# Half-contraction feed-forward chunks, two chunks per PSUM bank, and norm1 modulation on TensorE in one layer of a hybrid attention/S5 decoder

## The chip, the cores and the metric

The kernel runs on one core of a Trainium2 chip. The metric is the device time in microseconds (us) of one execution, as the median of several runs. Engines are named as in the profile: PE is TensorE (PEld its weight loads), DVE is VectorE, ACT is ScalarE, POOL is GpSimd, SP issues the transfers.

## The reference, cut to what matters

One layer, 256 tokens, width 2048, float32:

```
mod = silu(c) @ w_ada + b_ada                  # w_ada: 2048 x 12288, 100 MB
sh1, sc1, g1, sh2, sc2, g2 = split(mod, 6)
h = rms_norm(x, norm1_g) * (1 + sc1) + sh1
q, k, v, u = split(h @ w_in)                   # 2048 x 4096
attn = dilated_attention(qk_norm(q), qk_norm(k), v)
y = gelu(s5_mixer(u, ...)); ssm = y * sigmoid(y @ w_glu + b_glu)
x = x + g1 * (concat(rms_norm(attn), rms_norm(ssm)) @ w_out)     # 2048 x 2048
h2 = rms_norm(x, norm2_g) * (1 + sc2) + sh2
out = x + g2 * (square(relu(h2 @ w_ff1)) @ w_ff2)                # 2048 x 8192 x 2048
```

## The kernel before, in words

Activations lie transposed: channels on the 128 partitions, 256 tokens along the free dimension. Every product is made of float32 values split into a high and a low part of type fp32r: high x high, high x low and low x high. Weights come in tiles of 512 KB (128 partitions x 2 x 512). `raw` (L176) issues each transfer on SP's queue into one of five `raw` buffers; `split` (L172) makes the high part `wh` on ScalarE and the low part `wl` on VectorE, three buffers of each.

**The modulation.** w_ada has 24 blocks of 512 columns. Blocks 0 to 3 are sh1, 4 to 7 sc1, 8 to 11 g1, 12 to 15 sh2, 16 to 19 sc2, 20 to 23 g2. `ada_pieces` (L241) does a block in four pieces of 1 MB, which are two `raw` tiles each, or one larger tile where a ring of other buffers is set. A block in `PE_BLOCKS` (L42) goes to TensorE: per piece four matmuls against `cpad` at 32 columns each (L249, eight records per piece), and at the end a copy of the rows on ScalarE and column sums (L260). Any other block goes to VectorE: per raw tile one product with `cbc` whose sum is read out (L158). `ADA_ORDER` (L43) is the order of the blocks. Pieces are put between other work by `pump(n)` and `pump_at(i)` (L280, L581): `pump_at(i)` adds PUMPS[i] to a running sum and issues as many whole pieces; `until` stops it at that many pieces of the 96.

**The order of the work.** Norm 1; 8 pieces; `make_h(0)`; then the 32 blocks of w_in with S5 preparation, `make_h(1)` to `make_h(3)` and the scan between them (L607 to L650); attention and w_glu; `branch_scale`. w_out follows in two passes (L865 and L878) of eight `w_out_pair`, over the S5 half and the attention half of the contraction. A pair takes two weight tiles and two PSUM banks: each chunk of 128 output channels has a bank, whose columns 0 to 255 hold high times high plus low times high, and columns 256 to 511 high times low. Two additions per chunk on VectorE (L156, out XT, which is `z`) then bring both into z. The second pass also squares z on ScalarE (L883) and sums the squares with a matmul against ones (L886).

Then norm 2: the inverse root on VectorE (n2), its broadcast by matmul (L817), and `make_h2(kg)` (L899) for four chunks of channels each: on VectorE v = z * g2c * r2 (L905), on ScalarE the high part (L907), on VectorE the low part (L908). `make_h2(kg)` first pumps until 56 + 8 kg pieces, as it needs the blocks 12 + kg and 16 + kg.

The feed-forward part has 32 pairs of w_ff1 (64 chunks) with four weight tiles each, and w_ff2 in four groups G of eight pairs. `ff1_first` runs the first four pairs together in all eight banks (four `tr`, four `acc`), so that each quarter of h2 is used as soon as it is made. A pair's result is taken out in `ff1_out`: a copy on ScalarE and an addition on VectorE for each chunk, then the squared relu, the high part and the low part.

Tile places the instructions: it follows the program's order as priority but lets an instruction run ahead where its engine would be idle in its own simulated timeline. Each engine then takes its instructions strictly in the order so fixed.

Of the kernel before, what the change touches and what calls it, by code (L numbers as in the profile page):

```python
# [9 lines left out]
F32 = mybir.dt.float32  # L10
# [3 lines left out]
ALU = mybir.AluOpType  # L14
PSUM = bass.MemoryType.PSUM

P = 128
SEQ = 256
# [7 lines left out]
NB = 512  # L26
RAW = 5
RINGS = (('raw',), ('raw',), ('T0', 'PD', 'raw', 'raw'), ('T0', 'raw', 'raw'), ('U', 'raw'), ('WB0', 'U', 'raw', 'raw'))
PUMPS = (2.5, 2.75, 1.0, 1.5, 0.75, 0.75, 1.5, 1.25, 1.0, 2.0, 0.25, 2.75, 1, 0.75)

COLS = {}
_o = 0
# [6 lines left out]
NCOLS = _o  # L39

SUB = [0, 2, 1, 3]
PE_BLOCKS = (0, 4, 5, 7, 10, 11, 12, 16)  # L42
ADA_ORDER = (4, 0, 5, 1, 6, 2, 7, 3, 8, 9, 10, 11, 12, 16, 13, 17, 14, 18, 15, 19, 20, 21, 22, 23)  # L43


# [71 lines left out]
class _K:  # L117
# [5 lines left out]
    def t(self, tag, shape, dt=F32, bufs=1):  # L123
        self.n += 1
        return self.sb.tile(list(shape), dt, name=f"{tag}_{self.n}", tag=tag, bufs=bufs)
# [5 lines left out]
    def tr(self):  # L131
        self.n += 1
        return self.ps.tile([P, NB], F32, name=f"tr_{self.n}", tag="tr", bufs=4)
# [7 lines left out]
    def add(self, out, a, b, eng=None):  # L141
        return self.tt(out, a, b, ALU.add, eng)

    def sub(self, out, a, b, eng=None):
        return self.tt(out, a, b, ALU.subtract, eng)
# [8 lines left out]
    def stt(self, out, a, s, b, op0, op1, accum=None):  # L154
        if accum is None:
            self.nc.vector.scalar_tensor_tensor(out, a, s, b, op0=op0, op1=op1)  # L156
        else:
            self.nc.vector.scalar_tensor_tensor(out, a, s, b, op0=op0, op1=op1, accum_out=accum)  # L158

    def copy(self, out, a, scale=1.0):  # L160
        self.nc.scalar.activation(out, a, AF.Copy, scale=scale)  # L161
# [36 lines left out]
def _body(nc, tc, I, out, sb, ps):  # L198
    k = _K(nc, tc, I, out, (sb, ps))
    t, tr = k.t, k.tr  # L200
    mul, add, sub, ts, stt, copy = k.mul, k.add, k.sub, k.ts, k.stt, k.copy
    mm = nc.tensor.matmul
# [21 lines left out]
    cpad = t("cpad", [P, 16, 32])  # L224
# [356 lines left out]
    def pump_at(i, until=96):  # L581
        state["due"] += PUMPS[i]
        n = int(state["due"] + 1e-6)
        state["due"] -= n
        pump(n, until)
# [250 lines left out]
    def load_p(src):  # L836
        w = k.raw(src)
        hi = t("wh", [P, 2, 4, P], F32R, bufs=3)
        lo = t("wl", [P, 2, 4, P], F32R, bufs=3)
        flat = lambda v: v.rearrange("p e k n -> p e (k n)")  # L840
        k.split(flat(hi), flat(lo), w)
        return hi, lo

    def pair_part(pp, src, xs, first, last):
        hi, lo = load_p(src)
        for e in range(2):
            for kk in range(4):
                mm(pp[e], hi[:, e, kk], xs[kk].rearrange("p s n -> p (s n)"), start=first and kk == 0, stop=False)  # L848
            for kk in range(4):
                mm(pp[e][:, 0:SEQ], lo[:, e, kk], xs[kk][:, 0], start=False, stop=last and kk == 3)  # L850


    def w_out_pair(half, x8, np_):
        pp = [k.acc(), k.acc()]
        for kg in range(2):
            xs = [x8[:, 4 * kg + kk] for kk in range(4)]
            pair_part(pp, I["w_out"][np_, 2 * half + kg], xs, kg == 0, kg == 1)
        for e in range(2):
            c = 2 * np_ + e
            for s in (1, 0):  # L860
                stt(
                    z[:, c], pp[e][:, SEQ * s : SEQ * s + SEQ], mod[:, 32 + c : 33 + c], z[:, c], ALU.mult, ALU.add
                )

    for np_ in range(8):  # L865
        w_out_pair(1, xss, np_)
# [11 lines left out]
    for np_ in range(8):  # L878
        w_out_pair(0, xat, np_)
        if np_ % 2:  # L880
            pump_at(12, 80)
        sq = nsq[np_ // 4][:, 2 * (np_ % 4) : 2 * (np_ % 4) + 2]
        nc.scalar.activation(sq, z[:, 2 * np_ : 2 * np_ + 2], AF.Square)  # L883
        for e in range(2):
            for m in range(2):
                mm(  # L886
                    pn2[:, m : m + 1], sq[:, e, P * m : P * m + P], ones,
                    start=np_ + e + m == 0, stop=np_ + e + m == 9,
                )
# [9 lines left out]
    def make_h2(kg):  # L899
        pump(99, until=56 + 8 * kg)  # L900
        c4 = slice(4 * kg, 4 * kg + 4)
        stt(g2c[:, c4], mod[:, 64 + 4 * kg : 68 + 4 * kg], 1.0, col["n2g"][:, c4], ALU.add, ALU.mult)
        for c in range(4 * kg, 4 * kg + 4):
            v = nsq[c // 8][:, c % 8]
            stt(v, z[:, c], g2c[:, c : c + 1], r2, ALU.mult, ALU.mult)  # L905
            sh = mod[:, 48 + c : 49 + c]
            nc.scalar.activation(h2[c][:, 0], v, AF.Identity, bias=sh)  # L907
            stt(h2[c][:, 1], v, sh, h2[c][:, 0].bitcast(F32), ALU.add, ALU.subtract)  # L908


    y2 = [t("WB2", [P, 8, SEQ]), t("WB3", [P, 8, SEQ])]
    y2 = [y2[c // 8][:, c % 8] for c in range(16)]
    slots = [t(s, [P, 4, 2, SEQ], F32R) for s in ("HA", "U", "WB1", "HB", "V", "WB0")]
    xq = t("QK", [P, 2, 4, 2, SEQ], F32R)
    slots += [xq[:, 0], xq[:, 1]]

    def ff1_part(pp, np_, kg):
        pair_part(pp, I["w_ff1"][np_, kg], h2[4 * kg : 4 * kg + 4], kg == 0, kg == 3)

    def ff1_out(pp, np_):  # L920
        aa = slots[np_ // 2 % 8][:, 2 * (np_ % 2) : 2 * (np_ % 2) + 2]
        v = t("rows", [P, 2, SEQ], bufs=2)
        for e in range(2):
            copy(v[:, e], pp[e][:, SEQ : 2 * SEQ])
            add(v[:, e], pp[e][:, 0:SEQ], v[:, e])
        stt(v, v, 0.0, v, ALU.max, ALU.mult)
        copy(aa[:, :, 0], v)
        sub(aa[:, :, 1], v, aa[:, :, 0].bitcast(F32))

    def ff1(np_):  # L930
        pp = [k.acc(), k.acc()]
        if np_ % 2 == 0:
            pump(1)
        for kg in range(4):
            ff1_part(pp, np_, kg)
        ff1_out(pp, np_)

    def ff1_first():
        pps = [[tr(), tr()], [tr(), tr()], [k.acc(), k.acc()], [k.acc(), k.acc()]]
        for kg in range(4):  # L940
            make_h2(kg)
            for np_ in range(4):
                ff1_part(pps[np_], np_, kg)
                if kg < 3:
                    pump_at(13, 80)
        for np_ in range(4):
            ff1_out(pps[np_], np_)

    def ff2(G, np_):
        pp = [k.acc(), k.acc()]  # L950
# [14 lines left out]
            if G == 3:  # L965
                nc.sync.dma_start(out[c], y)

    ff1_first()
    for np_ in range(4, 8):
        ff1(np_)  # L970
    for G in range(4):
        if G < 3:
            for np_ in range(2):
                ff1(8 * G + 8 + np_)
        if G == 3:
            pump(99)
            for c in range(16):
                stt(y2[c], y2[c], mod[:, 80 + c : 81 + c], z[:, c], ALU.mult, ALU.add)
        for np_ in range(8):
            ff2(G, np_)  # L980
        if G < 3:
            for np_ in range(2, 8):
                ff1(8 * G + 8 + np_)
# [21 lines left out]
```

## Time and profile before

| | us |
|---|---|
| median of 3 runs | 1285.88 |
| lowest, highest | 1280.72, 1296.6 |
| profiled execution | 1299.06 |
| its span | 1297.3 |
| PE busy | 1198.6 (92%) |
| PEld busy | 993.7 (77%) |
| DVE busy | 921.8 (71%) |
| ACT busy | 582.0 (45%) |
| moved by DMA | 299.59 MB, mean 231 GB/s |

The profiled execution is one execution, and 1% above the median of the runs shown. Shares over the whole span say little here, as the stretches differ; the rows below are by stretch. A busy TensorE isn't TensorE at its peak: matmuls overlap, so their cost is read from start to start.

### The profile page before, as it was taken

What the parts mean: (1) busy time and instruction counts of PE and PEld (TensorE: products, weight loads), DVE (VectorE), ACT (ScalarE), POOL (GpSimd) and SP (SyncE); (2) the same over time, 40 slices, a digit from 0 to 9 for tenths busy, and PEclk for the clock granted to TensorE, in tenths of its full rate; (3) what the DMA queues carried; (4) which work ended last, traced back from release to release, by engine and by line L of the source; (5) the groups of instructions that cost most, each with busy time, mean ns of one, the idle gap of its engine ahead of it and who ended that gap; (6) DMA issues with size and microseconds to landing.
All of it is one profiled execution on the core that took longest, in us unless ns stands there. A gap on an engine that the chain in (4) does not pass through costs nothing.

```text
span 1297.3 us, 17972 instructions
## 1 busy us (share of the span) xinstructions
PE 1198.6 (92%) x6818; PEld 993.7 (77%) x6818; DVE 921.8 (71%) x1520; ACT 582.0 (45%) x807; POOL 13.0 (1%) x12
## 2 busy tenths in 40 slices
PE   5777999998987977949999999999999999999998
PEld 1355778865677866838888888888888888888887
DVE  9687678899555898877865556765566666667764
ACT  3579544322275533324544444443344443344432
POOL 3000000000000000000000000000000000000000
PEclk9788999999688897969999999999999999999999
DMA  9687898888544486748766666765677666667763
GB/s 345 228 271 259 337 341 314 286 313 289 196 149 162 149 302 213 255 154 275 242 220 188 189 217 224 248 192 184 190 233 239 224 183 191 205 235 248 241 211 96
DMA packets 82166, 299.59 MB, mean 231 GB/s; under 512 B 9120, under 2 KB 11424, under 8 KB 80288
## 3 DMA queue, kind: packets, MB, share of 16 engines
q1 hardware_dynamic: 82080, 298.45, 69.2%
q8 instruction: 53, 0.87, 0.3%
q14 instruction: 33, 0.27, 0.1%
HBM read 296.31 MB, written 2.10 MB: 230 GB/s over the span
## 4 chain that ended last, share of the span: by engine, by line
PE 76%; DVE 8%; DMA 7%; ACT 6%; issue 2%; SPq 0%; DVEq 0%; ACTq 0%
PE acc L848 37%; PE acc L850 18%; DMA raw<-w_ada 6%; PE acc L194 4%; PE acc L195 4%; PE acc L193 4%; DVE wl L136 2%; PE tr L249 2%; DVE raw L158 2%; PE acc L690 1%; ACT wh L161 1%; PE tr L553 1%; PE acc L686 1%; ACT TO L161 1%; PE tr L848 1%
## 5 line engine op out<-in xcount | busy, mean ns | idle before, releaser
L136 DVE TENSOR_TENSOR wl<-raw,wh 128x1024 fp32r<-128x1024 f32 x360 | 439.8, 1223 | 260.6 <-ACT wh L161 259.6
L161 ACT ACTIVATE wh<-raw 128x1024 fp32r<-128x1024 f32 x360 | 381.3, 1060 | 505.5 <-PE acc L848 347.2
L158 DVE SCALAR_TENSOR_TENSOR raw<-raw,cbc 128x1024 f32<-128x1024 f32 x112 | 136.6, 1222 | 53.7 <-DMA raw<-w_ada 53.1
L848 PE MATMUL acc<-CA,wh 128*128 128x512 f32 x608 | 167.0, 397 | 2.5 <-DVE XT L156 2.0
L848 PE MATMUL acc<-TO,wh 128*128 128x512 f32 x480 | 132.0, 396 | 0.6 <-DVE rows L136 0.6
L848 PE MATMUL acc<-QK,wh 128*128 128x512 f32 x384 | 107.4, 402 | 13.1 <-DVE QK L136 13.1
L848 PEld LDWEIGHTS acc<-CA,wh 128*128 128x128 f32 x608 | 104.7, 189 | 16.7 <-issue 2.2
L850 PEld LDWEIGHTS acc<-CA,wl 128*128 128x128 f32 x608 | 92.4, 188 | 13.1
L850 PE MATMUL acc<-CA,wl 128*128 128x256 f32 x608 | 96.1, 281 | 0.0
L848 PEld LDWEIGHTS acc<-TO,wh 128*128 128x128 f32 x480 | 82.5, 189 | 11.7 <-PE acc L850 0.8
L848 PEld LDWEIGHTS acc<-QK,wh 128*128 128x128 f32 x384 | 67.4, 193 | 22.4 <-issue 13.3
L850 PEld LDWEIGHTS acc<-TO,wl 128*128 128x128 f32 x480 | 73.3, 188 | 10.6
L850 PE MATMUL acc<-TO,wl 128*128 128x256 f32 x480 | 76.1, 281 | 0.0
L848 PE MATMUL acc<-WB,wh 128*128 128x512 f32 x256 | 69.8, 394 | 0.0
L850 PEld LDWEIGHTS acc<-QK,wl 128*128 128x128 f32 x384 | 58.3, 189 | 7.7
L850 PE MATMUL acc<-QK,wl 128*128 128x256 f32 x384 | 60.3, 279 | 0.0
L193 PE MATMUL acc<-wh,HA 128*128 128x512 f32 x128 | 48.6, 411 | 9.0 <-ACT wh L161 8.9
L194 PE MATMUL acc<-wl,HA 128*128 128x512 f32 x128 | 52.2, 408 | 0.0
L194 PE MATMUL acc<-wl,HB 128*128 128x512 f32 x128 | 50.7, 397 | 0.4 <-DVE wl L136 0.4
L195 PE MATMUL acc<-wh,HA 128*128 128x512 f32 x128 | 50.6, 401 | 0.0
L195 PE MATMUL acc<-wh,HB 128*128 128x512 f32 x128 | 50.0, 393 | 0.0
L848 PEld LDWEIGHTS acc<-WB,wh 128*128 128x128 f32 x256 | 43.7, 188 | 5.6
(269 smaller groups left out, 1763.5 us busy)
## 6 DMA issues: line engine op xcount, KB each, us to landing
raw<-w_ff SPq DMA_DIRECT2D x256, 512.0 KB, 4.3
raw<-w_ada SPq DMA_DIRECT2D x158, 512.0 KB, 5.2
raw<-w_in SPq DMA_DIRECT2D x64, 512.0 KB, 5.9
raw<-w_out SPq DMA_DIRECT2D x32, 512.0 KB, 4.8
U<-w_ada SPq DMA_DIRECT2D x8, 1024.0 KB, 7.3
XT<-xT SPq DMA_DIRECT2D x8, 512.0 KB, 5.8
T<-w_ada SPq DMA_DIRECT2D x8, 512.0 KB, 6.5
raw<-w_glu SPq DMA_DIRECT2D x8, 512.0 KB, 6.0
```

The lines of the kernel that those rows point to most:

```text
L136: return (eng or self.nc.vector).tensor_tensor(out, a, b, op=op)
L158: self.nc.vector.scalar_tensor_tensor(out, a, s, b, op0=op0, op1=op1, accum_out=accum)
L161: self.nc.scalar.activation(out, a, AF.Copy, scale=scale)
L193: mm(ps, xh, wh, start=start, stop=False)
L194: mm(ps, xh, wl, start=False, stop=False)
L195: mm(ps, xl, wh, start=False, stop=stop)
L249: mm(acc[32 * q : 32 * q + 32, :], cpad[:, 4 * g + q, :], raw[:, i, :], start=g == 0, stop=g == 3,)
L553: mm(pv[:, r - r2, ri], wb[r // 8][:, r % 8, ri], u2[:, :, r, :], start=True, stop=True)
L686: mm(pv[:, r - r8], toep[:, r].rearrange("p g s j -> p (g s j)"), u2[:, :, r, :], start=True, stop=False)
L690: mm(pv[pr, r - r8], ca[pr, r, ri].rearrange("p s j -> p (s j)"), H[pr, ri, r, :], start=False, stop=ri == 1,)
L848: mm(pp[e], hi[:, e, kk], xs[kk].rearrange("p s n -> p (s n)"), start=first and kk == 0, stop=False)
L850: mm(pp[e][:, 0:SEQ], lo[:, e, kk], xs[kk][:, 0], start=False, stop=last and kk == 3)
```

## The change

Five things are done.

1. `PE_BLOCKS` gains 1, 2, 3 and 6, so all of sh1 and sc1 is made on TensorE.
2. `pair_bank` puts two chunks into one bank: 256 columns each, to which all three products are added. It has 24 matmuls of 256 columns per weight tile, where `pair_part` has 8 of 512 and 8 of 256. `w_out_pair` uses it, with one bank and one addition into z per chunk.
3. `pump_at(12, 80)` in the second pass of w_out becomes `pump_at(12, 64)`, and PUMPS[13] goes from 0.75 to 0.5.
4. `make_h2` takes its v from two buffers of two chunks (`rows`) instead of from `nsq`.
5. `ff1_half` replaces `ff1_first`: eight banks take pairs 0 to 7 over the first half of the contraction (kg 0 and 1), 32 chunks in two rounds with pairs 8 to 15; each bank is copied to `part` in SBUF. `make_h2(2)` and `make_h2(3)` come only then. `ff1` finishes the first 16 pairs over kg 2 and 3 and adds `part` on VectorE, where a copy on ScalarE stood.

```diff
-PUMPS = (2.5, 2.75, 1.0, 1.5, 0.75, 0.75, 1.5, 1.25, 1.0, 2.0, 0.25, 2.75, 1, 0.75)
+PUMPS = (2.5, 2.75, 1.0, 1.5, 0.75, 0.75, 1.5, 1.25, 1.0, 2.0, 0.25, 2.75, 1, 0.5)
-PE_BLOCKS = (0, 4, 5, 7, 10, 11, 12, 16)
+PE_BLOCKS = (0, 1, 2, 3, 4, 5, 6, 7, 10, 11, 12, 16)
+    def pair_bank(bank, src, xs, first, last):
+        hi, lo = load_p(src)
+        for e in range(2):
+            o = bank[:, SEQ * e : SEQ * e + SEQ]
+            for kk in range(4):
+                mm(o, hi[:, e, kk], xs[kk][:, 0], start=first and e + kk == 0, stop=False)
+                mm(o, hi[:, e, kk], xs[kk][:, 1], start=False, stop=False)
+            for kk in range(4):
+                mm(o, lo[:, e, kk], xs[kk][:, 0], start=False, stop=last and e + kk == 4)
     def w_out_pair(half, x8, np_):
-        pp = [k.acc(), k.acc()]
+        bank = k.acc()
...
-            pair_part(pp, I["w_out"][np_, 2 * half + kg], xs, kg == 0, kg == 1)
+            pair_bank(bank, I["w_out"][np_, 2 * half + kg], xs, kg == 0, kg == 1)
         for e in range(2):
             c = 2 * np_ + e
-            for s in (1, 0):
-                stt(
-                    z[:, c], pp[e][:, SEQ * s : SEQ * s + SEQ], mod[:, 32 + c : 33 + c], z[:, c], ALU.mult, ALU.add
-                )
+            stt(z[:, c], bank[:, SEQ * e : SEQ * e + SEQ], mod[:, 32 + c : 33 + c], z[:, c], ALU.mult, ALU.add)
...
-            pump_at(12, 80)
+            pump_at(12, 64)
...
-            v = nsq[c // 8][:, c % 8]
+            if c % 2 == 0:
+                vv = t("rows", [P, 2, SEQ], bufs=2)
+            v = vv[:, c % 2]
...
+    pa = [t("WB2", [P, 4, NB]), t("WB3", [P, 4, NB]), t("PD", [P, 4, NB]), t("T0", [P, 2, NB])]
+    part = [pa[i // 4][:, i % 4] for i in range(14)] + [t("cpad", [P, NB]), t("apow", [P, NB])]
+    def ff1_half(base):
+        banks = [tr() for _ in range(4)] + [k.acc() for _ in range(4)]
+        for kg in range(2):
+            if base == 0:
+                make_h2(kg)
+            for i in range(8):
+                pair_bank(banks[i], I["w_ff1"][base + i, kg], h2[4 * kg : 4 * kg + 4], kg == 0, kg == 1)
+                pump_at(13, 80)
+        for i in range(8):
+            copy(part[base + i], banks[i])
+    def ff1(np_):
+        pp = [k.acc(), k.acc()]
+        if np_ % 2 == 0:
+            pump(1)
+        kgs = range(2, 4) if np_ < 16 else range(4)
+        for kg in kgs:
+            pair_part(pp, I["w_ff1"][np_, kg], h2[4 * kg : 4 * kg + 4], kg == kgs[0], kg == 3)
...
-            copy(v[:, e], pp[e][:, SEQ : 2 * SEQ])
+            if np_ < 16:
+                add(v[:, e], pp[e][:, SEQ : 2 * SEQ], part[np_][:, SEQ * e : SEQ * e + SEQ])
+            else:
+                copy(v[:, e], pp[e][:, SEQ : 2 * SEQ])
             add(v[:, e], pp[e][:, 0:SEQ], v[:, e])
...
-    ff1_first()
-    for np_ in range(4, 8):
+    ff1_half(0)
+    ff1_half(8)
+    make_h2(2)
+    make_h2(3)
+    for np_ in range(8):
         ff1(np_)
```

## Rows read from the trace of the kernel before

**Rows 1.** Busy by stretch: range, length; PE, PEld, DVE, ACT, POOL; clock, DMA, GB/s

```profile
57.00:130.00 73.00, 56.58 (x320) 42.05 (x319) 56.80 (x107) 61.67 (x122) 1.82 (x1) 0.86 0.80 271
130.00:252.00 122.00, 121.62 (x614) 97.70 (x613) 95.13 (x133) 56.72 (x75) 0.22 (x1) 1.00 0.91 332
...
430.00:495.00 65.00, 49.39 (x287) 42.90 (x285) 58.42 (x117) 26.41 (x41) 0.00 (x0) 0.92 0.75 251
495.00:548.00 53.00, 52.63 (x304) 46.40 (x304) 42.38 (x76) 19.33 (x21) 0.00 (x0) 0.94 0.68 229
548.00:574.00 26.00, 4.84 (x23) 4.18 (x23) 20.18 (x49) 7.45 (x16) 0.00 (x0) 0.59 0.69 239
...
620.00:1297.00 677.00, 672.82 (x3840) 587.62 (x3840) 435.07 (x567) 293.00 (x342) 0.00 (x0) 1.00 0.66 209
```

**Rows 2.** Chain that ended last, shares, of 57:130, 130:252, 430:495 and 548:574

```profile
by line: ACT TO L161 17.7%; ACT PD L161 12.8%; ACT wh L161 11.2%; PE tr L504 9.8%; DMA raw<-w_in 9.6%; ACT WB L161 9.3%; issue 7.1%; ACT XT L316 5.5%; PE acc L193 2.2%; PE acc L195 1.9%; ACT HA L161 1.8%; ACT HB L161 1.8%; DVE T L136 1.8%; 
...
by line: PE acc L194 27.8%; PE acc L195 27.0%; PE acc L193 26.9%; PE tr L553 11.7%; PE tr L249 2.4%; PE tr L504 1.4%; DVE wl L136 1.0%; ACT wh L161 0.9%; PE tr L260 0.6%; issue 0.5%; ACT QK L161 0.0%
...
by line: DMA raw<-w_ada 31.9%; DVE wl L136 19.7%; DVE raw L158 13.7%; DVE XT L156 11.9%; issue 11.5%; DVE U L156 4.4%; ACT WB L722 1.9%; ACT wh L161 1.5%; DVE adap L136 0.9%; DVE T L136 0.9%; ACT HB L161 0.6%; DVE QK L136 0.5%; DVE rbc L818
...
by line: DMA raw<-w_ada 63.1%; DVE raw L158 14.5%; DVE V L156 12.2%; issue 8.7%; DVE WB L156 6.1%; DVE wl L136 4.7%; DVE XT L156 3.4%; PE tr L848 3.0%; DVE TO L156 1.6%; DVE adap L136 0.8%; DVE mod L136 0.1%; DVEq L158 0.1%
```

**Rows 3.** Timeline of PE, feed-forward part: start, length, instructions [idle before]

```profile
573.40 2.07 PE L848 MATMUL tr<-TO,wh 128*128 128x512 f32 x4 [9.02 <-DVE TO L156]
...
880.24 1.10 PE L848 MATMUL acc<-V,wh 128*128 128x512 f32 x4
...
883.04 1.10 PE L848 MATMUL acc<-WB,wh 128*128 128x512 f32 x4
```

**Rows 4.** Timeline of PE in w_glu

```profile
372.64 0.28 PE L798 MATMUL acc<-TO,wh 128*128 128x256 f32 x1
...
378.34 0.28 PE L798 MATMUL acc<-TO,wh 128*128 128x256 f32 x1
```

**Rows 5.** Busy by stretch, columns as rows 1: w_glu, feed-forward part

```profile
372.64:378.34 5.70, 5.70 (x51) 5.70 (x50) 2.87 (x4) 3.86 (x6) 0.00 (x0) 1.00 0.14 22
880.00:890.00 10.00, 10.00 (x60) 8.76 (x59) 5.42 (x6) 3.44 (x4) 0.00 (x0) 1.00 0.58 195
```

**Rows 6.** Groups by line: count | busy us, mean ns | idle before

```profile
L136 DVE TENSOR_TENSOR wl<-raw,wh 128x1024 fp32r<-128x1024 f32 x360 | 439.8, 1223 | 260.6 <-ACT wh L161 259.6
L161 ACT ACTIVATE wh<-raw 128x1024 fp32r<-128x1024 f32 x360 | 381.3, 1060 | 505.5 <-PE acc L848 347.2 <-DMA raw<-w_in 46.6 <-issue 32.6
...
L156 DVE SCALAR_TENSOR_TENSOR XT<-acc,mod,XT 128x256 f32<-128x256 f32 x64 | 29.2, 478 | 0.5 <-PE acc L850 0.3
```

**Rows 7.** Stretch 548 to 574, line L158 alone: DVE busy (x), clock, DMA, GB/s

```profile
548.00:574.00 26.00, 8.61 (x14) 0.59 0.69 239
```

**Rows 8.** Timeline of PE and DVE between w_out and the feed-forward part

```profile
547.46 0.63 PE L850 MATMUL acc<-QK,wl 128*128 128x256 f32 x4
...
556.71 1.87 PE L886 MATMUL tr<-ones,WB 128*128 128x1 f32 x8 [6.43 <-ACT WB L883]
...
563.16 1.23 PE L817 MATMUL tr<-ident,n 128*128 128x128 f32 x4 [4.58 <-DVE n L136]
...
568.04 3.25 DVE L156 SCALAR_TENSOR_TENSOR V<-XT,g2c,rbc 128x256 f32<-128x256 f32 x8
```

**Rows 9.** Chain by time, 140:197: a w_ada piece and a block's sums on PE

```profile
149.68 0.99 PE tr L249 x8
...
183.16 0.79 PE tr L260 x8
```

**Rows 10.** Timeline of DVE: two evictions of ff1 one after the other

```profile
619.97 0.75 DVE L136 TENSOR_TENSOR rows<-acc,rows 128x256 f32<-128x256 f32 x2
...
622.97 0.75 DVE L136 TENSOR_TENSOR rows<-acc,rows 128x256 f32<-128x256 f32 x2
```

**Rows 11.** Waits in 575:1290: us in total, times, longest

```profile
DVE raw L158 <- DMA raw<-w_ada: 30.8, 27, 3.5
```

More of the change, by code (lines that the diff above doesn't have):

```diff
@@ L908, in make_h2 @@
             stt(h2[c][:, 1], v, sh, h2[c][:, 0].bitcast(F32), ALU.add, ALU.subtract)
-    y2 = [t("WB2", [P, 8, SEQ]), t("WB3", [P, 8, SEQ])]
-    y2 = [y2[c // 8][:, c % 8] for c in range(16)]
     slots = [t(s, [P, 4, 2, SEQ], F32R) for s in ("HA", "U", "WB1", "HB", "V", "WB0")]
@@ L915, in _body, with ff1_slot @@
     slots += [xq[:, 0], xq[:, 1]]
[L917 to L921, printed above, removed]
+    def ff1_slot(np_):
+        return slots[np_ // 2 % 8][:, 2 * (np_ % 2) : 2 * (np_ % 2) + 2]
+    pa = [t("WB2", [P, 4, NB]), t("WB3", [P, 4, NB]), t("PD", [P, 4, NB]), t("T0", [P, 2, NB])]
[17 more added lines that the diff above has]
+            pair_part(pp, I["w_ff1"][np_, kg], h2[4 * kg : 4 * kg + 4], kg == kgs[0], kg == 3)
+        aa = ff1_slot(np_)
         v = t("rows", [P, 2, SEQ], bufs=2)
         for e in range(2):
-            copy(v[:, e], pp[e][:, SEQ : 2 * SEQ])
+            if np_ < 16:
+                add(v[:, e], pp[e][:, SEQ : 2 * SEQ], part[np_][:, SEQ * e : SEQ * e + SEQ])
+            else:
+                copy(v[:, e], pp[e][:, SEQ : 2 * SEQ])
             add(v[:, e], pp[e][:, 0:SEQ], v[:, e])
@@ L928, in ff1_out @@
         sub(aa[:, :, 1], v, aa[:, :, 0].bitcast(F32))
[L930 to L947, printed above, removed]
     def ff2(G, np_):
@@ L966, in ff2 @@
                 nc.sync.dma_start(out[c], y)
-    ff1_first()
-    for np_ in range(4, 8):
+    ff1_half(0)
[3 more added lines that the diff above has]
+    for np_ in range(8):
         ff1(np_)
+    y2 = [t("WB2", [P, 8, SEQ]), t("WB3", [P, 8, SEQ])]
+    y2 = [y2[c // 8][:, c % 8] for c in range(16)]
     for G in range(4):
```

## The prediction

> **What bounds the kernel now.** I cut the span into stretches by the table of busy times [rows 1] and read for each the chain that ended last [rows 2]. The reader should see two kinds of stretch. From 620 us to the end TensorE is busy 672.8 of 677 us at full clock, and the stretch 130 to 252 us is the same (121.6 of 122, the chain 82% in the w_in matmuls of L193 to L195). There only fewer or cheaper matmuls help, and every matmul added costs its length. In the other stretches TensorE waits: 57 to 130 us is led by ScalarE (busy 61.7 of 73 us; its copies, pad writes and modulation are some 60% of the chain), 430 to 495 us by VectorE (58.4 of 65 us) with the w_ada transfers that it waits for, and 548 to 574 us, between w_out and the feed-forward part, by those transfers almost alone (63% of the chain; TensorE busy 4.8 of 26 us).
>
> The feed-forward part has 256 weight tiles of 512 KB. Two groups of hi and lo matmuls, which is one tile, take 883.04 - 880.24 = 2.80 us [rows 3], so 256 tiles need 717 us. From the first matmul at 573.40 [rows 3] that ends at 1290, and the span ends at 1297.3. So there is nothing to win inside that part; what the change can win lies before 574 us.
>
> **Two chunks per bank.** 64 weight tiles (32 in w_out, 32 in the first feed-forward halves) go from 8 matmuls of 512 columns and 8 of 256 to 24 of 256: the same columns, 8 more weight loads each. The trace has this pattern already. In w_glu (L798 to L800) every matmul has 256 columns and a load of its own: 48 start between 372.64 and 378.34 [rows 4], 118.8 ns each, so 24 take 2.85 us against 2.80. That is 0.05 us x 64 = 3.2 us; 0.8 for the second half of w_out, which TensorE fills (52.6 of 53 us [rows 1]), 1.6 for the feed-forward halves, and nothing for the first half of w_out, where VectorE leads. The load engine is busy 8.76 of 10 us in the feed-forward part and 5.70 of 5.70 in w_glu [rows 5]: the new pattern has no reserve left, but it doesn't overrun.
>
> The Trainium skill ("TensorE: Matmul & The Clock Gate", section "LDWEIGHTS (loading the stationary operand)") gives a load as its columns over 1.2 GHz, 107 ns for 128. If none of the 512 extra loads were hidden, the sum by that would be an estimated 55 us more. By the row, loads and matmuls overlap, and the sum takes 3.2 us or less. The skill's advice to judge TensorE by the busy share of its loads ("Perfetto Trace Analysis", section "Identifying the Most-Contended Engine") agrees with the rows in that this pattern stands at the limit.
>
> **Evictions of w_out.** Before, each chunk takes two additions into z from PSUM, 64 of 478 ns [rows 6]; now one. In the first half (the loop over w_out_pair(1, ...)) 16 go, 7.6 us of VectorE [rows 6]. It leads there, but part of its time is waiting for w_ada, which returns as waiting. The ends are 0 and -7.6; I take -4. In the second half TensorE is full, and the 16 that go gain nothing.
>
> **The gap before the feed-forward part.** Summing PUMPS along the program, 69 pieces (of 96; one is 1 MB of w_ada, for a VectorE block two L158 products) have been pumped by the end of the first half of w_out, in both kernels. Before, the second half adds 4, and the products that run ahead from ff1_first add more: 14 instructions of L158 with their reads lie in 548 to 574 us, seven products of 1.23 us each [rows 7]. After, the 64 in pump_at(12, 64) is already passed, so the second half pumps none; the next piece comes behind the first feed-forward tile, then every second tile. By the order of the five raw buffers, which are given out in program order, I expect two of these pieces before the gap, and three or four products in it instead of seven. The gap has three stops for TensorE [rows 3, 8]: 6.43 us for the last square (the z additions stand behind L158 in VectorE's order), 4.58 us for the norm, and 9.02 us for h2. In the last, VectorE makes 12 products v (L905, 3.25 us for eight, so 4.9 for twelve) before the first low part. After, v lives in two buffers of two chunks, so at most four come first, 1.6 us instead of 4.9: -3.3. Of the first two stops, 11 us, half goes with half the products: -5.5. Together -8.8, say -9. The ends are 0 (other pieces fill the gap again) and -16: of the 25.3 us between the end of the last w_out matmul (547.46 + 0.63) and 573.40, about 9 are left for two z additions, the square, eight norm sums (1.87 us), the norm with its broadcast (1.23 us) and the first product.
>
> **Norm1 modulation on TensorE.** Blocks 1, 2, 3 and 6 leave VectorE: 32 products of 1.23 us [rows 7], 39 us. On TensorE a piece is 8 records in 0.99 us, and a block ends with column sums of 0.79 us [rows 9], so a block costs 4 x 0.99 + 0.79 = 4.75 us there, and four 19 us. By the same sum of PUMPS, 18 pieces are pumped when make_h(1) is reached, so blocks 1 and 6 fall mostly before 130 us, where TensorE has 16 us idle: nothing. Blocks 2 and 3 fall in the full stretch 130 to 252: +9.5. Against that, the chain of 57 to 130 holds 9.6% of 73 us, 7.0 us, in one w_in transfer, and the buffer for it is freed by an L158 product; with that gone I take 5.5 back. ScalarE, the leader there, loses no work and gains two copies of rows. Together +4; the ends are -7 (idle time hides all of it) and +14 (nothing comes back, and half of blocks 1 and 6 shows too). The piece's wait for its transfer moves from VectorE's queue, where the low parts of w_in stand behind it, to TensorE's, where the w_in matmuls do; as the stretch is led by ScalarE and then by TensorE, I cost that at nothing beside the ends.
>
> **The halves.** Each of two rounds over eight banks ends with eight copies of 128x512 on ScalarE, about half of a weight copy of 1060 ns [rows 6] each. Seven can run while the last bank fills. The next weight copy may queue behind the eighth: about 0.5 + 1.06 + a low part, 2.5 us, for each of two turns. The ends are 0 and 5; three weight buffers speak for the lower: +1.
>
> Then 16 passes of ff1 contract over half: two weight tiles, 5.60 us on TensorE, but a whole eviction, in which an addition on VectorE replaces a copy on ScalarE. Before, two additions, the square, the low part of the result and a weight tile's low part repeat in 3.00 us [rows 10]. A half pass has one more low part of a weight tile (1.22 [rows 6]) and two more additions (0.75), 4.97 us; two passes 9.9, and the piece pumped for every two adds two products, 2.46: 12.4 us against 11.2 on TensorE. With the mean wait for w_ada in this part, 30.8 / 27 = 1.14 us per product [rows 11], it is 14.7. So VectorE leads by 1.2 to 3.5 us for each two passes: 4.8 to 14 in the first eight, 3.6 to 10.5 in the six after the first ff2 round. Three weight tiles in hand cover 8.4 us each time, so 0 to 7.7 shows: +3. With no cover it is 24. The pieces that were moved back here (27 by the sum of PUMPS, against 23) are otherwise hidden under TensorE.
>
> **Sum.** -4 + 0.8 - 9 + 4 + 1.6 + 1 + 3 = -2.6 us. Against the profiled execution of 1299.06 us that is 1296; this execution was 1% above the median of the three runs, 1285.88, so I set the forecast at 1283.
>
> **Rivals.**
> A. The gap closes to its floor (-16), VectorE's relief in w_out counts in full (-7.6), and idle time hides the moved blocks (0): 0.8 - 7.6 - 16 + 0 + 1.6 = -21, 1265, and 1258 with the early gain of 7. For it: both stretches wait for w_ada on VectorE [rows 2]. Against: the five buffers are given out in order, so new pieces run ahead into the gap.
> B, slower: the half passes make VectorE the bound. It decides from the point where two passes take more than 11.2 us on VectorE for longer than 8.4 us of cover: 24 instead of 3 us gives 1304. For it: 12.4 to 14.7 against 11.2. Against: the waits often fall where VectorE would be idle anyway.
> C. Nothing moves: the pieces fill the gap again, and the sum is +6, 1292. The 25 us would then still show.
> D. The extra loads aren't hidden: 512 loads of 0.15 us (8.76 us for 59 [rows 5]) make 76 us, 1359. The rows of w_glu speak against it. This is what the skill's load time would do without overlap.
>
> **Chances.** Forecast 0.50, A 0.22, B 0.14, C 0.12, D 0.02. Two per cent, about what a measurement of this kernel can tell from no change, are 26 us: below 1260 or above 1312. Half of A is below: faster 0.11. D and a third of B are above: slower 0.07. Within: 0.82. The range reaches from A's centre to B's, 1264 to 1304; what is left out is half of A, half of B and D, 0.2.
>
> **What would show it.** Right: w_out tiles and first feed-forward halves at 2.85 us a tile; first feed-forward matmul some 16 us after the last of w_out instead of 25; few L158 there; TensorE without stops through the 32 half tiles; VectorE above 90% in ff1(0) to ff1(7) with short stops; the stretch to the scan a few us later. Wrong: a gap still above 20 us (C); stops of TensorE for VectorE between ff1 passes that sum above 10 us (B); the scan earlier than before (A).

## The result: slower by 3.7%, most of it before the scan

| | before | after |
|---|---|---|
| median, us | 1289.99 (4 runs) | 1338.39 (4 runs) |
| lowest, highest | 1280.72, 1296.6 | 1329.88, 1342.0 |
| profiled execution, its span | 1299.06, 1297.3 | 1337.88, 1336.0 |

The ratio is 1.037, with an interval of [1.028, 1.046]: 48 us slower, where I had forecast 1283 and a range to 1304. The first lines of the page of after, with the chain that ended last:

```profile
PE 1235.5 (92%) x7490; PEld 1028.7 (77%) x7490; DVE 881.7 (66%) x1443; ACT 583.3 (44%) x797; POOL 13.0 (1%) x12
...
PE 64%; DMA 16%; DVE 11%; ACT 5%; issue 4%; SPq 0%; DVEq 0%; ACTq 0%
```

VectorE lost 40 us of work, as the change says, and TensorE gained 37. The share of transfers in the chain is 16%. Where that comes from shows by stretch. The busy times of the two stretches of after that answer to [rows 1] (range, length; PE, PEld, DVE, ACT, POOL; clock, DMA, GB/s), and the chain of the second:

```profile
57.00:130.00 73.00, 61.97 (x329) 36.48 (x324) 34.78 (x58) 46.12 (x87) 1.81 (x1) 0.84 0.70 239
130.00:252.00 122.00, 111.10 (x539) 77.13 (x538) 45.68 (x56) 61.06 (x97) 0.00 (x0) 0.99 0.72 251
...
by line: DMA raw<-w_in 26.1%; DMA T<-w_ada 16.2%; PE acc L194 9.8%; PE acc L195 8.9%; PE tr L249 8.8%; DVE wl L136 8.0%; PE acc L193 7.3%; ACT wh L161 6.1%; issue 2.9%; ACT PD L161 2.7%; DVE T L158 1.1%; DVE raw L158 0.9%; PE tr L260 0.6%; 
```

From 130 to 252 us the chain was 82% w_in matmuls [rows 2]. Now these three lines have 26%, and transfers of w_in and w_ada 42%. The transfers move 251 GB/s there where they moved 332 [rows 1]: bandwidth is not what is short, and the waits of SP's queue, shown further down, have them start late. VectorE is busy 45.7 of 122 us. The first matmul of `state_in` (L553) stands late in the w_in stage and serves as its mark; first before, then after (timeline of PE: start, length):

```profile
237.41 14.40 PE L553 MATMUL tr<-PD,WB 128*128 128x64 f32 x128
```

```profile
276.35 14.40 PE L553 MATMUL tr<-PD,WB 128*128 128x64 f32 x128
```

It comes 38.9 us later, and the span is 38.7 us longer. In this pair of profiles, then, what changes behind it sums to nothing, and the main question is what happens between 57 and 276 us, where only one part of the change acts: blocks 1, 2, 3 and 6 on TensorE.

All differences below are ratio times 1290, with the interval of the ratio. A profile is one execution; that of before was 9 us above its median, so shifts between profiles and between medians differ by some us.

### The profile page after: what moved, and what is told of

It is laid out like the page before. It is cut to its first block, busy times and chain, and to the rows that moved or that the text cites. A ratio compares the mean times of both kernels' runs of the same rounds, so it can differ in the third digit from the quotient of the medians.

```text
span 1336.0 us, 19220 instructions
## 1 busy us (share of the span) xinstructions
PE 1235.5 (92%) x7490; PEld 1028.7 (77%) x7490; DVE 881.7 (66%) x1443; ACT 583.3 (44%) x797; POOL 13.0 (1%) x12
## 4 chain that ended last, share of the span: by engine, by line
PE 64%; DMA 16%; DVE 11%; ACT 5%; issue 4%; SPq 0%; DVEq 0%; ACTq 0%
PE acc L848 28%; PE acc L850 14%; DMA raw<-w_ada 10%; DMA raw<-w_in 3%; DVE wl L136 3%; PE tr L249 3%; DVE raw L158 2%; PE acc L194 2%; PE acc L857 2%; PE acc L860 2%; PE acc L858 2%; PE acc L195 2%; PE acc L193 2%; DMA T<-w_ada 1%; ACT wh L161 1%
## 5 line engine op out<-in xcount | busy, mean ns | idle before, releaser
L848 PE MATMUL acc<-CA,wh 128*128 128x512 f32 x512 | 140.8, 400 | 5.9 <-DVE rows L136 4.9
L158 DVE SCALAR_TENSOR_TENSOR raw<-raw,cbc 128x1024 f32<-128x1024 f32 x86 | 105.2, 1224 | 61.4 <-DMA raw<-w_ada 60.6
L249 PE MATMUL tr<-raw,cpad 128*32 128x512 f32 x288 | 57.9, 693 | 16.3 <-DMA raw<-w_ada 16.3
L848 PE MATMUL acc<-TO,wh 128*128 128x512 f32 x256 | 70.3, 396 | 0.0
L848 PE MATMUL acc<-QK,wh 128*128 128x512 f32 x256 | 69.8, 394 | 0.0
L195 PE MATMUL acc<-wh,HB 128*128 128x512 f32 x128 | 51.0, 398 | 0.0
L193 PE MATMUL acc<-wh,HB 128*128 128x512 f32 x128 | 48.5, 407 | 2.6 <-ACT wh L161 2.6
L848 PEld LDWEIGHTS acc<-QK,wh 128*128 128x128 f32 x256 | 43.9, 189 | 5.7
L848 PEld LDWEIGHTS acc<-TO,wh 128*128 128x128 f32 x256 | 43.9, 188 | 5.7
L850 PEld LDWEIGHTS acc<-WB,wl 128*128 128x128 f32 x256 | 39.3, 188 | 5.6
L850 PEld LDWEIGHTS acc<-TO,wl 128*128 128x128 f32 x256 | 39.1, 188 | 5.7
```

The source lines that it names most:

```text
L193: mm(ps, xh, wh, start=start, stop=False)
L195: mm(ps, xl, wh, start=False, stop=stop)
L249: mm(acc[32 * q : 32 * q + 32, :], cpad[:, 4 * g + q, :], raw[:, i, :], start=g == 0, stop=g == 3,)
```

## Experiments

### Which part of the change

**The blocks put back** (after, with the old PE_BLOCKS) and **the blocks alone** (before, with the new PE_BLOCKS):

```diff
-PE_BLOCKS = (0, 1, 2, 3, 4, 5, 6, 7, 10, 11, 12, 16)   # after -> first run
+PE_BLOCKS = (0, 4, 5, 7, 10, 11, 12, 16)
```

> The whole change, but blocks 1, 2, 3 and 6 of w_ada go back to VectorE. Three theories of the 48 us. Hold: a w_ada piece for TensorE keeps its raw buffer until TensorE comes to it in its queue, so the w_in transfers behind it start late. Time: the four blocks simply add TensorE work to a stretch that TensorE fills. Others: the banks, evictions and half passes cost it. By hold and by time the first state matmul (L553) is back at about 237 us and the median at 1280 to 1290; by others it stays above 1325.

> The kernel before with only blocks 1, 2, 3 and 6 moved to TensorE. By hold and by time about 39 us more than before, 1325 to 1332, with the first L553 near 276 us; by others no change, 1285 to 1295.

Measured: with the blocks put back 1286.7, ratio 0.9986 [0.9948, 1.0024], the first state matmul at 238.4; the blocks alone 1341.8, 1.0409 [1.0361, 1.0457], the first state matmul at 276.7. So the blocks are the whole loss (+53 us by the runs, +39 by the profile), and the rest of the change is worth -2 us [-7, +3]. The blocks alone came out above the 1325 to 1332 expected. After and the blocks put back differ in the four blocks only: their profiles are 38.0 us apart at the first state matmul (276.35 and 238.37) and 47.6 at the end (spans 1336.0 and 1288.4). So some 10 us of the loss lie behind that mark, spread over the rest, and no run here says what they are; the profile of before hides them, as it was itself a long execution.

**Two blocks at a time.** The kernel before, with blocks 1 and 6, then with blocks 2 and 3 on TensorE:

```diff
+PE_BLOCKS = (0, 1, 4, 5, 6, 7, 10, 11, 12, 16)
```
```diff
+PE_BLOCKS = (0, 2, 3, 4, 5, 7, 10, 11, 12, 16)
```

> The kernel before with only blocks 1 and 6 moved to TensorE, the two that are worked on before about 140 us, while ScalarE leads. The forecast took them at nothing, as TensorE has 16 us idle there. By hold they are the greater part: the traces of the change show the first transposes of L504 39 us late already; 1315 to 1330.

> The kernel before with only blocks 2 and 3 moved to TensorE, in the stretch that TensorE fills. The forecast took +9.5 for them, by their matmuls. By hold 10 to 20 us, 1297 to 1310, as the buffers are held there too but weights are in hand.

Measured: 1318.8 (1.0216 [1.0145, 1.0287]) and 1321.2 (1.0246 [1.0184, 1.0308]); the first state matmul at 264.4 and 258.9. Each pair costs about the same, 28 and 32 us. I had put blocks 1 and 6 at nothing, and 2 and 3 at 9.5; the theory of kept buffers had 2 and 3 at 1310 at most.

### How much of it is TensorE's time

**The added matmul time alone.** The four blocks stay on VectorE; TensorE does their matmuls and column sums as well, on `cbc`, which is resident, and the sums go into a spare tile. Nothing that TensorE adds waits for a transfer or keeps a buffer.

```diff
+                if extra:
+                    for q in range(4):
+                        mm(acc[32*q : 32*q + 32, :], cpad[:, 4*j + q, :], cbc[:, NB*q : NB*q + NB], start=j == 0, stop=j == 3)
```

**A quarter of the columns.** The blocks alone, where TensorE multiplies only 128 of the 512 columns of these four blocks:

```diff
-     acc[32*q : 32*q + 32, :], cpad[:, 4*g + q, :], raw[:, i, :],
+     acc[32*q : 32*q + 32, 0:w], cpad[:, 4*g + q, :], raw[:, i, 0:w],     # w = 128 for blocks 1, 2, 3, 6
```

> The kernel before; the blocks 1, 2, 3 and 6 stay on VectorE and give the result, but TensorE does the matmuls of four blocks as well, against cbc, which is resident, with the copy of the rows and the column sums, whose result is thrown away. So TensorE has the added work of the change, and no raw buffer waits for it. By time most of the 39 us appears, 1320 or more; by hold only what falls in the full stretch, 0 to 10 us, 1290 to 1300.

> The kernel before with blocks 1, 2, 3 and 6 on TensorE, where their matmuls take 128 of the 512 columns (the other 384 columns of these blocks are left out and repeated from the first 128). The raw buffers are held until TensorE comes to them, as in the change, but its work on a piece falls from 0.99 to about 0.3 us. By hold 25 to 39 us more than before remain, 1315 to 1330; by time at most a third of it, 1295 to 1303.

Measured: the added time alone 1310.2, 1.0168 [1.0139, 1.0198], first state matmul at 247.4; a quarter of the columns 1318.8, 1.0229 [1.0196, 1.0262], at 260.2. The first lies between the ranges of the two theories. The whole matmul time costs 22 us if no transfer hangs on it (10 of them up to the first state matmul); a part of it costs 30 us if one does. So there is a second cause besides time.

### What hangs on the transfers

**Buffers of their own.** If the shared `raw` buffers are kept too long, give the four blocks two buffers of 512 KB in cbc's place, and load cbc only before block 8, which first needs it then:

```diff
+        if own:
+            for i in range(2):
+                raw = t("cbc", [P, 2, NB], bufs=2)
+                nc.sync.dma_start(raw, ...)
```

> The kernel before with blocks 1, 2, 3 and 6 on TensorE, but their pieces land in two 512 KB buffers of their own (the place of cbc, which is loaded only when block 8 needs it), so the five raw buffers are left to w_in and to the blocks that had them before. TensorE's work is that of the change. By hold only the cost of the work remains, as in e3: 10 to 25 us over before, 1297 to 1313. If what costs is the order in TensorE's queue and not the buffers, it stays at 1330 or more.

Measured: 1348.1, 1.044 [1.0373, 1.0507]; first state matmul at 286.4. Not better, so by what was expected the kept buffers alone are not the cause. The waits of SP's queue in 57 to 290 us (us in total, times, longest) offered another reason:

```profile
SPq L248 <- PE tr L267: 30.1, 24, 2.9
```

SP stood 24 times at the issue of a piece whose buffer TensorE had not freed, with the w_in transfers behind it.

**Another queue.** The same with the pieces' transfers issued on GpSimd, and the blocks alone with their transfers on GpSimd:

```diff
-                nc.sync.dma_start(raw, ...)
+                nc.gpsimd.dma_start(raw, ...)
```

> The kernel before with blocks 1, 2, 3 and 6 on TensorE and with two buffers of their own for these pieces, as in the run with own buffers (1348.1), but these pieces' transfers are issued on GpSimd's queue and no longer on SP's. In that run the profile shows SP's queue stopped 30.1 us in 24 places between 57 and 290 at the issue of such a piece, until TensorE had freed its buffer; every transfer of w_in behind it waited too. Theory queue (the loss beyond the added matmul time comes from SP's queue, which stands still until TensorE has worked off an earlier piece): those 30 us go, the first state matmul, at 290 there, comes at 250 to 265, and the time is 1305 to 1325, near the 1310 of the kernel that only adds the matmul time. Theory wait (TensorE takes its instructions in order and itself waits for the piece's transfer, whoever issues it): no change, 1338 or more.

> The kernel before with blocks 1, 2, 3 and 6 on TensorE (1341.8 so far), with the transfers of these four blocks issued on GpSimd's queue; they still land in the shared raw buffers, which go round in the program's order. Theory queue: w_in transfers no longer stand behind a piece whose buffer TensorE has not freed, but one in three or so still wants that same buffer next, so part of the loss returns: 1315 to 1330. Theory hold (the shared buffer itself is kept until TensorE comes to the piece): little returns, 1332 or more. Theory wait: 1338 or more here and in the run with own buffers.

Measured: 1350.4 (1.0455 [1.0405, 1.0506]) and 1347.1 (1.0429 [1.0368, 1.0489]); the first state matmul at 286.2 and 283.4. SP's queue was not the cause. In the first of them GpSimd's queue shows who is late, and the matmuls of the four blocks (128 records) show what they cost (groups by line: busy, mean ns, idle before; first of the added time alone, then of own buffers with GpSimd's queue):

```profile
L272 PE MATMUL tr<-cbc,cpad 128*32 128x512 f32 x128 | 17.5, 628 | 0.0
```

```profile
POOL cbc L248 <- PE tr L267: 200.9, 24, 67.6
...
L267 PE MATMUL tr<-cbc,cpad 128*32 128x512 f32 x128 | 30.8, 633 | 8.1 <-DMA cbc<-w_ada 8.1
```

GpSimd waited 201 us for TensorE to free a buffer, and TensorE 8.1 us for these pieces: the data mostly lay there and TensorE came late. And the same 128 records took 30.8 us instead of 17.5.

**Whole pieces.** The reason for that price stands in the timelines. Here the four records of a half piece alone, and the eight of a whole one (of the next run), both where the granted clock is 1.00:

```profile
90.08 1.05 PE L267 MATMUL tr<-cbc,cpad 128*32 128x512 f32 x4
```

```profile
89.72 1.06 PE L264 MATMUL tr<-cbc,cpad 128*32 128x512 f32 x8
```

The four matmuls of a piece go to four column groups and run side by side; two of them alone take as long as four. The Trainium skill ("TensorEngine Tiling (Array Packing)", section "Key Properties") says that different tiles of the array can load and multiply in parallel, and these two rows agree. So a piece costs 1 us if its halves stand together in TensorE's order and 2 us if w_in matmuls come between. The run: the piece lands whole, 1 MB in one buffer of its own:

```diff
+            raw = t("cbc", [P, 4, NB])
+            nc.gpsimd.dma_start(raw, src.rearrange("p (a n) -> p a n", a=4))
```

> As the run with own buffers and GpSimd's queue (1350.4), but a piece of blocks 1, 2, 3 and 6 now lands whole, 1 MB in the one buffer of 8 KB per partition in cbc's place, and not as two halves. In the traces so far eight records of a whole piece take TensorE 0.99 us, and the four records of a half piece that stands alone take 0.98 us; in that run 23 of 31 groups were lone halves, and the pieces took 41.2 us of TensorE before the first state matmul, where 24 whole pieces would take 25. Theory halves (the price of a piece is set by halves that land apart): some 16 us come back, the first state matmul at 265 to 275 for 286, the time 1325 to 1337. Theory wait (TensorE stands in its order at pieces whose transfer is late, and a single buffer makes that worse): lone halves go, but the stops grow by as much, 1345 or more.

Measured: 1367.1, 1.0573 [1.0517, 1.063], the slowest of all; first state matmul at 300.3. Groups by line and TensorE's waits (us in total, times, longest) in 57 to 310 us:

```profile
L264 PE MATMUL tr<-cbc,cpad 128*32 128x512 f32 x128 | 19.9, 697 | 17.9 <-DMA cbc<-w_ada 17.9
...
PE tr L264 <- DMA cbc<-w_ada: 17.9, 7, 5.6
PE acc L193 <- ACT wh L161: 16.6, 7, 6.7
```

The price of the matmuls came back, from 30.8 to 19.9, as the halves theory has it; but with one buffer TensorE now stands at the pieces (17.9 us) and at w_in (16.6), and loses more than that. These four runs show that the pieces' own time is mis-sized, and that TensorE stopping for a transfer is dear. They don't clear the kept buffers: each trades them for lone halves or for stops.

**The two causes apart.** So the suspicion was put into the kernel before by itself. The four blocks stay on VectorE; behind each of their products TensorE makes a matmul of a single column, in one run of the raw tile (so that the buffer stays taken until TensorE comes by), in the other of the sum that VectorE has written (TensorE depends on the same transfers, but VectorE frees the buffer):

```diff
                     stt(rf, rf, 1.0, cbc[:, o : o + n], ALU.mult, ALU.mult, accum=part[:, i, j : j + 1])
+                    if touch is not None:   # blocks 1, 2, 3, 6
+                        mm(touch[0:32, 0:1], cpad[:, 0, :], raw[:, 0, 0:1], start=True, stop=True)
```
```diff
+                        mm(touch[0:32, 0:1], cpad[:, 0, :], part[:, i, j : j + 1], start=True, stop=True)
```

> The kernel before, with blocks 1, 2, 3 and 6 on VectorE as ever; behind each product of a raw tile TensorE makes one more matmul of a single column of that tile into a spare bank (32 in all, some 0.1 us each, so 3 us at most). So TensorE has to have come by before the buffer is free. Theory hold (buffers kept until TensorE comes by): 1305 to 1330, the first state matmul at 250 to 265 for 237. Theory wait (TensorE stands at the transfer of the tile): the same here. Theory price (it is the pieces' own time on TensorE, lone halves and the lower clock, and not the dependence): 1290 to 1296, the first state matmul at 238 to 242.

> As the run before this one, but the one column that TensorE reads is the sum that VectorE's product has written, and not the raw tile: TensorE stands in its order behind the same transfers, but VectorE alone frees the buffers. Theory wait: as slow as the touch of the raw tile, 1305 to 1330. Theory hold: back at 1290 to 1296, the first state matmul at 238 to 242, with the touch of the raw tile slow. Theory price: both at 1290 to 1296.

Measured: the touch of the raw tile 1319.3, 1.0203 [1.0136, 1.0271]; the touch of the sum 1300.7, 1.0058 [1.0024, 1.0092]. First the raw tile, then the sum: a wait of SP's queue in 57 to 237 us, and the first state matmul:

```profile
SPq L178 <- PE tr L272: 31.3, 13, 8.8
...
254.31 14.40 PE L556 MATMUL tr<-PD,WB 128*128 128x64 f32 x128
```

```profile
SPq L178 <- DVE raw L158: 31.9, 26, 3.2
...
244.64 14.40 PE L556 MATMUL tr<-PD,WB 128*128 128x64 f32 x128
```

32 matmuls of one column, about 4 us of TensorE, cost 26 us if they keep the buffer and 7 if they only depend on it, their own time included. In the first SP waits 31 us for TensorE in 13 places, up to 8.8 us each; in the second VectorE frees the buffers at 26 places, never later than 3.2. The kept buffer is worth 19 us by the runs, the difference, or some [9, 28] with both intervals. At the first state matmul of the two profiles the difference is 10 us. The touch of the sum stays above the 1290 to 1296 that the theory of kept buffers expected, so that theory is not all of it.

**Both together.** The added time alone, with the touch of the raw tiles on top:

> The kernel that adds the matmul time alone (blocks 1, 2, 3 and 6 stay on VectorE, TensorE does their matmuls on resident data as well) with the touch of each raw tile by TensorE added: added time and kept buffers together, VectorE's work as before. If the two parts add up: 1294 + 22 + 25 - 3 = 1335 to 1345, the first state matmul at 258 to 270. If they hide each other (TensorE's stops are filled by the added matmuls): 1315 to 1325, at 247 to 255, and the rest of the 1342 of the moved blocks has another cause, lone half pieces first.

Measured: 1333.2, 1.0363 [1.0274, 1.0451], first state matmul at 271.4. By the runs the two add up: 22 + 26 = 48, and together 47 [35, 58]; the blocks alone have 53 [47, 59]. What is left, some 6 us, lies within the intervals; the lone halves are a candidate for it. At the first state matmul of the profiles the two are 10 and 17 us, together 34, and the blocks alone 39: how exactly they add up is known to some 10 us only.

**The wait itself.** Both parts show in what ScalarE's copies of the w_in weights waited for (47 or 48 copies in each run, from 57 us to the first state matmul; us in total, times, longest). Before, after, and own buffers with GpSimd's queue:

```profile
ACT wh L161 <- DMA raw<-w_in: 27.5, 15, 3.4
```

```profile
ACT wh L161 <- DMA raw<-w_in: 46.9, 22, 5.5
```

```profile
ACT wh L161 <- PE acc L195: 61.9, 26, 7.7
ACT wh L161 <- DMA raw<-w_in: 27.8, 8, 9.7
```

In the kernels where TensorE keeps no more raw buffers than before (before, the time alone, the touch of the sum) the wait for w_in transfers is 24 to 32 us; where it keeps more (after, the blocks alone, the touch of the raw tile, time and touch) it is 42 to 47. With own buffers, on either queue, it is back at 28 to 29: w_in is no longer late. There ScalarE waits 49 to 62 us for TensorE to come to older weights (14.7 before), so TensorE itself is behind, with 41 us of pieces in the account below.

**The account of TensorE.** From its timeline: for every row the time from its start to the next row's start, without the idle that the next row shows, summed by line from 57 us to the first state matmul.

| us | before | time alone | touch of raw | touch of sum | time and touch | blocks alone | own, GpSimd | whole piece |
|---|---|---|---|---|---|---|---|---|
| first state matmul | 237.4 | 247.4 | 254.3 | 244.6 | 271.4 | 276.7 | 286.2 | 300.3 |
| pieces, touches | 8.8 | 25.0 | 12.6 | 12.3 | 31.8 | 32.9 | 41.2 | 28.3 |
| column sums | 2.5 | 5.9 | 2.5 | 2.5 | 6.9 | 5.8 | 6.3 | 6.3 |
| w_in matmuls | 137.8 | 138.8 | 145.8 | 141.7 | 144.4 | 144.2 | 145.1 | 149.9 |
| S5 matmuls | 14.8 | 11.6 | 14.6 | 14.4 | 11.6 | 14.8 | 10.4 | 11.3 |
| stops | 16.8 | 9.4 | 22.1 | 17.0 | 20.1 | 22.2 | 26.7 | 47.9 |

With the time alone, 20 us of work are added and up to the first state matmul 10 of them fall into stops and into the S5 transposes: the stops shrink from 16.8 to 9.4. With the pieces themselves the stops don't shrink but grow to 22.2, the same w_in matmuls take 6 us more, and the pieces take 24 instead of 16. In the blocks alone the granted clock is 0.95 over this stretch, where before it was full from 130 us on [rows 1]:

```profile
130.00:237.00 107.00, 98.43 (x475) 68.19 (x473) 35.93 (x39) 51.60 (x83) 0.00 (x0) 0.95 0.71 247
```

The clock can be only a part of why the w_in matmuls are slower: in the trace of after the granted clock in the same stretch is 0.98, and by the same account they take 144.7 us there. The rest of these 6 us stays open.

### The rest of the change

**Two chunks per bank in w_out alone**: `pair_bank` and the new `w_out_pair` in the kernel before.

> The kernel before with two chunks per bank in w_out alone; the feed-forward part and the blocks of the modulation stay as before. My sum has -4 + 0.8 for this: about 1287 for a before of 1290, most of it in the second half of w_out, where VectorE falls behind. Theory gap: w_out's end comes some 15 us earlier here too (460.8 for 481.1 was the start of the second half's bound in the run with the old blocks), but the wait for the transfers of w_ada behind it takes it back, and the first feed-forward matmul comes at 568 to 576 as before: 1284 to 1292. Theory w_out (the evictions were the bound there): the first feed-forward matmul comes 10 us or more earlier and the time is 1275 to 1282.

Measured: 1292.1, 0.9979 [0.9935, 1.0024], -3 us [-8, +3]. In its profile, an execution 8 us under its median, TensorE's timeline at the change to the feed-forward part is:

```profile
546.22 1.23 PE L817 MATMUL tr<-ident,n 128*128 128x128 f32 x4 [8.93 <-DVE n L136]
556.98 2.05 PE L848 MATMUL tr<-TO,wh 128*128 128x512 f32 x4 [9.54 <-DVE TO L156]
```

The feed-forward part begins 16 us earlier in this profile than in that of before [rows 8], which the medians don't bear out; what can be read is that the stops ahead of it are as long as they were (8.9 and 9.5 us for 4.6 and 9.0). The gap is not closed by the banks.

**The last pieces moved.** With the blocks put back, the 16 pieces that were pumped one for every two passes of ff1 go between the pairs of ff2:

```diff
-        if np_ % 2 == 0:        # in ff1
-            pump(1)
+        if G < 3 and np_ % 3 < 2:   # in ff2
+            pump(1)
```

> The change without the moved blocks (as e1), and the last 16 pieces of w_ada are issued between the pairs of ff2 instead of between those of ff1. In e1 the feed-forward part takes some 13 us more than its matmuls, with stops of TensorE for VectorE among the half passes. If VectorE is the bound there, by evictions plus the products of w_ada, most of it goes: 1275 to 1282. If the stops come from the evictions alone or from the banks, 1284 to 1288.

Measured: 1282.8 (12 runs), 0.9934 [0.9899, 0.9968]: 9 us [4, 13] faster than before, the only version here that beats both kernels, and just above the 1275 to 1282 expected if VectorE is the bound there. The stretch 620 to 720 us, with ten of the 16 half passes, first with the blocks put back, then with the pieces moved:

```profile
620.00:720.00 100.00, 95.64 (x616) 86.94 (x615) 81.42 (x127) 46.34 (x55) 0.00 (x0) 0.98 0.72 241
```

```profile
620.00:720.00 100.00, 100.00 (x640) 90.44 (x639) 75.24 (x110) 47.20 (x56) 0.00 (x0) 1.00 0.68 217
```

With fewer products VectorE falls from 81 to 75 us, and TensorE's stops are gone.

## Why the prediction was wrong, and where it was right

**The step that failed is the norm1 modulation on TensorE**: +4 in the sum, with ends of -7 and +14; measured +53 [47, 59]. Four things in it were wrong:

- *"Blocks 1 and 6 fall mostly before 130 us, where TensorE has 16 us idle: nothing."* Blocks 1 and 6 cost 28 us. TensorE's idle time there was time in which w_in had not come. With the time alone half of the added work was hidden by it up to the first state matmul, and the runs still give 22 us at the end; with the pieces themselves the w_in transfers come later still, and the idle time is there again.
- *The price of 0.99 us a piece* [rows 9] holds for whole pieces (25.0 us for 24 in the run of the time alone). In the blocks alone 24 pieces take 32.9 us, 1.37 each, since some halves are issued apart. The row of eight records hid this; the four-record rows of the same line in the trace of before (0.98 us at 159.19 and at 176.86 us) would have shown it.
- *"The piece's wait for its transfer moves from VectorE's queue, ... to TensorE's, ... I cost that at nothing beside the ends."* That dependence is worth at most 7 us [3, 12], by the touch of the sum, whose own matmuls take some 4 of them. A bound from the rows was to be had: the products of VectorE wait 1.14 us each [rows 11], for 32 tiles 37 us with nothing hidden.
- *"With that gone I take 5.5 back"*: I asked what freed the buffer of that transfer, found an L158 product, and took it for gone. But the buffer then waits for TensorE's matmul of the piece, which stands behind w_in matmuls that wait for a w_in transfer, which waits for a buffer. That loop is how I read the kept buffer, which the two touch runs put at 19 us, some [9, 28]. The waits of after agree with it:

```profile
SPq L178 <- DVE wl L136: 66.3, 25, 8.7
SPq L178 <- PE tr L249: 33.4, 20, 5.2
```

(SP's queue in 57 to 237 us; before had 54.8 us and 15.7 in these two, and 26.0 for L158, which was never longer than 3.2.)

**The rest of the sum** was -6.6 us (-4 + 0.8 - 9 + 1.6 + 1 + 3); the blocks put back give -2 [-7, +3], so as a sum it lies at the edge of what was measured and is not refuted. Its terms:

- w_out, -3.2: -3 [-8, +3] by its own run. Not refuted, and too small to be confirmed.
- The gap, -9, from 25.3 to 16 us: with the blocks put back it is 12.9, from the end of the last w_out matmul to the first of the feed-forward part:

```profile
537.45 0.63 PE L860 MATMUL acc<-QK,wl 128*128 128x256 f32 x4
541.01 1.86 PE L893 MATMUL tr<-ones,WB 128*128 128x1 f32 x8 [2.92 <-ACT WB L890]
548.15 1.22 PE L817 MATMUL tr<-ident,n 128*128 128x128 f32 x4 [5.27 <-DVE n L136]
550.95 1.01 PE L857 MATMUL tr<-TO,wh 128*128 128x256 f32 x3 [1.58 <-ACT TO L916]
554.06 0.58 PE L858 MATMUL tr<-TO,wh 128*128 128x256 f32 x1 [2.10 <-DVE TO L156]
```

  The stop for the last square falls from 6.4 to 2.9, and that for h2 from 9.0 to 1.6 and 2.1: both as argued, the second further, while the norm's stays at 5.3 [rows 8]. As w_out alone leaves the gap open, this gain is not the banks' of w_out; no run parts the pumps, the two buffers of v and the new halves.
- The feed-forward part, +5.6 (1.6 + 1 + 3): from its first matmul to the end it takes 737.5 us with the blocks put back, for 723.9 before: +13.6, of which TensorE is busy 5.4 more and stops 8.2 more. TensorE's waits of this part in which the half passes show (us in total, times, longest):

```profile
PE acc L848 <- DVE rows L136: 4.2, 2, 3.5
PE acc L848 <- DVE adap L136: 0.8, 1, 0.8
```

  These are 5.0 us of stops, where the sum had 3 and allowed 7.7 (its working counts 14 of the 16 half passes; two more follow the first eight directly). The other stops are the 2.1 for h2 above and 1.8 for the low parts of weights in the first halves. With the pieces moved the two waits are gone and the part takes 731.8, +7.9. So rival B's mechanism was there, at a fifth of its 24 us: VectorE does lead in the half passes, and it is the piece pumped there that decides it, as the working said. The 13.6 ate what the gap gave, 12.4.

**The rivals.** None was the case. B ended on the right side, but for another place. The rival that I did not write was the one at the edit with the most engines in it: an engine that is the bound becomes the one that frees a shared buffer.

**What stays open.** Own buffers end the lateness of w_in and yet gain nothing: with two of them TensorE has 41 us of pieces, many as lone halves, and with one it stops; two buffers for whole pieces were not tried. Open too are the 10 us behind the first state matmul. Nor are the two parts of the touch of the sum apart, the wait itself and the changed order of instructions; Tile makes a new order for each of these kernels.

## What to carry over

Before a consumer is moved to another engine, ask who frees the buffer afterwards, and what stands ahead of that instruction in its engine's order: where a shared ring feeds the engine that is the bound, an engine beside it that frees the buffers quickly is worth more than its share of work shows (here some 19 us). Idle time that exists because a transfer is late is no cover for work that makes the transfer later. Matmuls that run side by side in column groups have to be issued together; priced by the row, look for the rows with half the count.

## What the hardware showed that I had not expected

- Two matmuls of 128x512 in column groups of 32 took as long as four: 1.05 us for four records, 1.06 us for eight, both at a granted clock of 1.00; 128 records took 17.5 us issued whole and 30.8 us as lone halves.
- 32 matmuls of one column, 4 us of TensorE in all, cost 26 us where each kept a buffer until TensorE came to it, and 7 us where VectorE freed the buffers.
